# A weight scan's loads: issued by GpSimd into shared tiles, or by ScalarE into four tiles of its own

## The chip, the cores and the metric

The kernel runs on one core of one Trainium2 chip. The metric is the device time of one execution in microseconds (us). A core has five engines that run side by side, each in its own order: TensorE (PE in the profile; its weight loads are PEld), VectorE (DVE), ScalarE (ACT), GpSimd (POOL) and SyncE (SP). They meet at semaphores. Transfers between HBM and the on-chip memory are issued by SP, POOL or ACT, go into the issuing engine's own queue, and are then moved by the core's 16 DMA engines, which all queues share. An engine that has to wait before it issues a transfer holds up everything behind it in its own order.

## What is computed

Two layers of a diffusion backbone, on 1024 latent tokens and 256 context tokens of width 1024. Each layer is a mixer followed by a feed-forward part with gate, up and down weights (hidden width 2816 = 22 blocks of 128). Cut to what matters:

```python
def ada_mod(cond, w, b):
    m = (jax.nn.silu(cond) @ w + b)[..., None, :]
    return jnp.split(m, 6, axis=-1)

def swiglu(u, w_gate, w_up, w_down):
    return (jax.nn.silu(u @ w_gate) * (u @ w_up)) @ w_down
...
for i in range(DEPTH):
    sh1, sc1, g1, sh2, sc2, g2 = ada_mod(c, ada_w[i], ada_b[i])
    ...
    h_lat = h_lat + g2 * swiglu(modulate(rms_norm(h_lat, norm2_g[i]), sh2, sc2),
                                ffn_w_gate[i], ffn_w_up[i], ffn_w_down[i])
return rms_norm(h_lat, final_g)
```

## The kernel before

The program is one straight list of instructions for each engine. The code below is run once, tile by tile; a scheduler then sets each engine's order, hands out the slots of the tile pools and puts in the semaphore waits. `self.follow(ins)` ties what is issued inside it behind `ins` on the same engine.

**The stage.** The change acts in the feed-forward part of the first layer, method `ffn(0, ...)`. Its gate and up products of the latent tokens are done in Strassen-Winograd form: a loop over 11 units `i`, each with two blocks of 128 hidden features. A unit has 7 products for gate and 7 for up (`wino_steps`), each product 12 matmuls of 128x512 in f16 (line 1983), so 168 matmuls. VectorE and ScalarE make the weight operands of a unit: ScalarE the scaled high part (line 1842), VectorE the remainder (line 1843), VectorE the sums of weight blocks (lines 1961 to 1969). ScalarE copies partial results out of PSUM (line 1988) and applies Silu (lines 2127, 2129). VectorE adds partial results (lines 1997, 2007, 2012), multiplies gate by up and forms the sums for the next matrix product (lines 2084 to 2090, method `finish`). For the down weights of a unit, VectorE makes four sums (lines 2044 to 2047, method `sums`).

**Three side jobs** are woven into the units, so as to use engines that have room:

- `scan`: the second layer's gate and up weights (44 blocks of 128x1024) are read once, to get a sum of absolute values for each, from which their f16 scale follows later. Each block is loaded into a tile and ScalarE takes Abs with an accumulated sum (line 1813). It keeps four blocks ahead, and `ffn` advances it four times in a unit.
- `ada_group`, called `todo` in `ffn`: the modulation vectors `silu(c) @ ada_w`. A block of 128x1024 of `ada_w` is loaded by GpSimd, and VectorE takes four dot products with it (line 565, two for `c_ctx` and two for `c`), here called a **dot group**. Units 0 to 7 do three such blocks, the later ones two.
- `finish` and `sums` write their results to DRAM (`d<-g`, `d<-tk`, `d<-s`) by GpSimd, through `ldr`, line 338.

**The shared tiles.** Scan blocks and `ada_w` blocks both live in the pool `p4` (`S4()`, tag `s4`, shown as `s` in the profile), which has 21 tiles of 128x1024 f32. In this stage 14 of them hold the layer's input operands (28 pairs of 128x512 in f16, two pairs a tile), 2 hold the conditioning vectors, and 5 are left. The scheduler gives a tile that comes free to whichever request stands next, and the request waits for the tile's last reader.

**The order on GpSimd.** All loads of the two jobs and all the writes stand in one row on GpSimd, and each waits there for its own tile or its own data.

```python
self.p4 = ent(tc.tile_pool(name="p4", bufs=21))
def lda(self, out, in_):
    self.nc.scalar.dma_start(out, in_)
def ldr(self, out, in_):
    self.last_ldr = self.nc.gpsimd.dma_start(out, in_).ins
```

Below, line 347 is the plain matmul of `mm`, lines 351 and 353 are `split`, 332, 335 and 338 are the issues of `ld` (SP), `lda` (ACT) and `ldr` (POOL).

Of the kernel before, what the change touches and what calls it, by code (L numbers as in the profile page):

```python
# [13 lines left out]
AF = mybir.ActivationFunctionType  # L14
# [244 lines left out]
class Builder:  # L259
# [1536 lines left out]
        nc.vector.tensor_scalar(ad[:, m * 8:m * 8 + 16], ad[:, m * 8:m * 8 + 16], t[:, 1:2], None, op0=MUL)  # L1796
        self.xinv = t[:, 0:1]

    def scan(self, key, tiles, ahead=4):

        nc = self.nc
        n = len(tiles)
        sums = self.C(2 * n)
        st = []
        for k in range(n + ahead):
            if k < n:
                t = self.S4()
                self.ldr(t, tiles[k])
                st.append(t)
            if k >= ahead:  # L1810
                t, i = st.pop(0), k - ahead
                with self.follow(self.last_hi):
                    nc.scalar.activation(t, t, AF.Abs, accum_out=sums[:, i:i + 1])
            yield
        self.wsc[key] = sums

# [1159 lines left out]
```

## Time and profile before

| what | value |
|---|---|
| time, median of 3 | 2927.53 us (2925.7 and 2940.76 the others) |
| the profiled execution's own time | 2929.4 us |
| its span in the profile | 2927.6 us |
| PE busy | 2759.0 us, 94% |
| VectorE busy | 2100.2 us, 72% |
| ScalarE busy | 1428.6 us, 49% |
| GpSimd busy | 565.0 us, 19% |
| mean granted clock of TensorE | 0.979 |

A row of the timeline is: start in us, length in us, engine, line, operation, out<-in, shape, count, and in brackets how long the engine had been idle and what ended that. A row of waits is: who waited, for whom, us in total, times, longest. A row of windows is: the stretch, its length, then busy time and instruction count of PE, PEld, DVE, ACT and POOL, the granted clock, the DMA engines' share and GB/s. By windows, the stretch before this stage (0 to 890 us) has 817.77 us of PE, the stretch of the down product behind it (1395 to 1610 us) 212.61 us in 215, and the second feed-forward part (2340 to 2927 us) 573.22 us in 587.

### The profile page before, as it was taken

To read this page: it belongs to the slowest core of one execution; us is meant where nothing else is said; L and a number is where in the kernel's file an instruction comes from. 1 tells how busy PE (TensorE), PEld (TensorE's weight loads), DVE (VectorE), ACT (ScalarE), POOL (GpSimd) and SP (SyncE) were. 2 spreads that over 40 slices of the span, in tenths; PEclk is the share of its full clock that TensorE was granted. 3 is DMA by queue.
4 is the path that set the end of the run, shared out by engine and by line. 5 is a ranking of instruction groups with operands and counts; after the bars stand their busy time and mean duration, and the time that the engine had idled before them with its cause. 6 is when DMAs were issued, how large, how long until landed. Compare 5 with 4: busy or idle time off the path is not lost. (4 is left out here: it accounts for less than half of the span.)

```text
span 2927.6 us, 43743 instructions
## 1 busy us (share of the span) xinstructions
PE 2759.0 (94%) x15570; PEld 1999.4 (68%) x15570; DVE 2100.2 (72%) x3683; ACT 1428.6 (49%) x2445; POOL 565.0 (19%) x921
## 2 busy tenths in 40 slices
PE   7999888999999988889999999999999999999998
PEld 3877677788896433334787988898987444444887
DVE  5678788768777776777778635787877876775546
ACT  3434235442685433345346434777865553443434
POOL 1210234341001212123111001333322012222000
PEclk9999999999999999999999999999999999999999
DMA  7355546755655655568997534878875335665664
GB/s 257 108 159 178 164 134 197 242 185 195 239 169 198 227 200 198 201 234 302 336 311 251 159 130 119 194 189 195 202 236 196 115 126 191 223 207 202 229 194 137
DMA packets 304936, 580.42 MB, mean 198 GB/s; under 512 B 82760, under 2 KB 129546, under 8 KB 304718
## 3 DMA queue, kind: packets, MB, share of 16 engines
q1 hardware_dynamic: 234894, 367.34, 40.1%
q0 software_dynamic: 66976, 205.57, 20.6%
q10 hardware_dynamic: 2848, 4.72, 0.4%
q8 instruction: 123, 2.02, 0.3%
q14 instruction: 95, 0.78, 0.1%
HBM read 430.17 MB, written 119.80 MB: 188 GB/s over the span
## 5 line engine op out<-in xcount | busy, mean ns | idle before, releaser
L1983 PE MATMUL ps<-s,s 128*128 128x512 f16 x2280 | 528.9, 387 | 60.9 <-ACT tk L1988 29.4
L1983 PEld LDWEIGHTS <-s 128*128 128x128 f16 x2640 | 260.5, 99 | 392.8 <-issue 73.3
L347 PE MATMUL ps<-s,wh 128*128 128x256 f32 (+1 forms) x1784 | 414.1, 334 | 8.2 <-ACT wh L351 5.3
L347 PEld LDWEIGHTS ps<-s,wh 128*128 128x128 f32 x1784 | 300.5, 191 | 43.3 <-ACT wh L351 6.8
L347 PE MATMUL ps<-s,wl 128*128 128x256 f32 (+1 forms) x892 | 273.0, 332 | 5.8 <-DVE wl L353 5.8
L351 ACT CAST s<-s 128x1024 fp32r<-128x1024 f32 (+2 forms) x192 | 172.7, 927 | 201.3 <-DMA s<-d 183.7
L2177 PE MATMUL ps<-s,s 128*128 128x512 f32 (+1 forms) x1000 | 258.2, 384 | 3.6 <-DVE s L353 3.3
L347 PE MATMUL pq<-s,wh 128*128 128x512 f32 (+1 forms) x840 | 255.2, 384 | 0.3 <-ACT wh L351 0.3
L347 PE MATMUL ps<-s,s 128*128 128x65 f16 (+4 forms) x2748 | 228.1, 234 | 14.9 <-DMA s<-tk 4.8
L353 DVE TENSOR_TENSOR s<-s,s 128x1024 fp32r<-128x1024 f32 (+2 forms) x170 | 190.7, 1154 | 70.3 <-ACT s L351 70.0
L1983 PE MATMUL ps<-s,hl 128*128 128x512 f16 x924 | 216.6, 385 | 1.2 <-ACT hl L1842 1.2
L2177 PEld LDWEIGHTS ps<-s,s 128*128 128x128 f32 x1000 | 184.3, 188 | 42.8 <-DVE s L353 6.4
L353 DVE TENSOR_TENSOR wl<-ws,wh 128x1024 fp32r<-128x1024 f32 (+1 forms) x102 | 121.4, 1192 | 120.7 <-ACT wh L351 116.2
L338 POOL DMA_DIRECT2D d<-s x245 | 133.3, 545 | 380.4 <-DVE s L1699 87.5
L1983 PEld LDWEIGHTS <-hl 128*128 128x128 f16 x1056 | 104.5, 99 | 129.6 <-issue 7.6
L351 ACT CAST wh<-ws 128x1024 fp32r<-128x1024 f32 (+1 forms) x102 | 103.5, 1016 | 168.0 <-PE ps L347 89.1
L347 PEld LDWEIGHTS ps<-s,wl 128*128 128x128 f32 x892 | 168.1, 192 | 24.4 <-DVE wl L353 7.6
L347 PEld LDWEIGHTS pq<-s,wh 128*128 128x128 f32 x840 | 149.3, 189 | 22.3 <-ACT wh L351 1.1
L347 PE MATMUL pq<-s,wl 128*128 128x512 f32 (+1 forms) x420 | 158.8, 378 | 0.0
L1842 ACT ACTIVATE s<-t,c 128x512 f16<-128x512 f32 x176 | 117.6, 713 | 71.8 <-DVE t L1962 54.9
L2177 PE MATMUL ps<-s 128*128 128x512 f32 (+1 forms) x500 | 149.5, 386 | 0.6 <-ACT s L351 0.6
L347 PEld LDWEIGHTS ps<-s,s 128*128 128x128 f32 (+1 forms) x828 | 129.3, 192 | 26.8 <-ACT t L2513 3.2
(523 smaller groups left out, 5385.0 us busy)
## 6 DMA issues: line engine op xcount, KB each, us to landing
s<-d SPq DMA_DIRECT2D x283, 256.0 KB, 4.1
d<-s POOLq DMA_DIRECT2D x229, 256.0 KB, 3.9
s<-in_down SPq DMA_DIRECT2D x150, 256.0 KB, 6.2
s<-in_ada_w POOLq DMA_DIRECT2D x64, 512.0 KB, 6.1
ws<-in_up SPq DMA_DIRECT2D x44, 512.0 KB, 4.3
ws<-in_gate SPq DMA_DIRECT2D x42, 512.0 KB, 3.7
d<-s SPq DMA_DIRECT2D x60, 256.0 KB, 2.3
d<-g POOLq DMA_DIRECT2D x56, 256.0 KB, 3.4
```

Of the source, the lines that this page charges most:

```text
L338: self.last_ldr = self.nc.gpsimd.dma_start(out, in_).ins
L347: self.last_mm = self.nc.tensor.matmul(o, l, r, start=st, stop=sp).ins
L351: self.last_hi = nc.scalar.copy(hi, src).ins
L353: self.last_lo = eng.tensor_tensor(lo, src, hi.bitcast(F32), SUB).ins
L1842: self.last_hi = self.nc.scalar.activation(hi, src, AF.Copy, scale=s).ins
L1983: nc.tensor.matmul(ps, x[:, sl], y, start=first and j == 0 and x is wh and y is xh, stop=j == 3 and x is wl, skip_group_check=True)
L2177: m = nc.tensor.matmul(acc[j][:, c0:c1], x[:, sl], y[:, xs], start=first and k == 0, stop=last and k == 2, skip_group_check=True)
```

## The change

`scan` takes four tiles of the pool once, at its start, and goes round them. A block's load is issued by ScalarE (`lda`, line 335), behind the Abs that read the tile's previous block, and inside the same `follow` as the Abs. The parameter `ahead` goes; four blocks ahead stay four. Nothing else is edited; the method is two lines shorter, so that lines behind it count two less (line 1843 becomes 1841, 565 stays).

```diff
-    def scan(self, key, tiles, ahead=4):
+    def scan(self, key, tiles):
...
-        st = []
-        for k in range(n + ahead):
-            if k < n:
-                t = self.S4()
-                self.ldr(t, tiles[k])
-                st.append(t)
-            if k >= ahead:
-                t, i = st.pop(0), k - ahead
-                with self.follow(self.last_hi):
-                    nc.scalar.activation(t, t, AF.Abs, accum_out=sums[:, i:i + 1])
+        st = [self.S4() for _ in range(4)]
+        for k in range(n + 4):
+            t = st[k % 4]
+            with self.follow(self.last_hi):
+                if k > 3:
+                    nc.scalar.activation(t, t, AF.Abs, accum_out=sums[:, k - 4:k - 3])
+                if k < n:
+                    self.lda(t, tiles[k])
             yield
```

The instructions of the engines move with it. GpSimd's row in the middle of the stage, before (`in_gate` is a scan load, `in_ada_w` a load for a dot group, `d` a write to DRAM):

```order
L338 DMA s_2637_10629<-in_gate 128x1024
L338 DMA s_2639_10662<-in_gate 128x1024
L338 DMA d_7414<-s_2582_10374 128x512
L338 DMA s_2644_10721<-in_gate 128x1024
L338 DMA d_7416<-s_2557_10153 128x512
L338 DMA s_2649_10740<-in_ada_w 128x1024
L338 DMA d_7418<-tk_10388 128x512
L338 DMA s_2654_10750<-in_ada_w 128x1024
```

The same place on GpSimd after the change:

```order
L338 DMA d_7412<-g_10258 128x512
L338 DMA s_2638_10734<-in_ada_w 128x1024
L338 DMA d_7415<-tk_10288 128x512
L338 DMA d_7414<-s_2571_10363 128x512
L338 DMA d_7416<-s_2549_10145 128x512
L338 DMA d_7418<-tk_10377 128x512
L338 DMA s_2643_10744<-in_ada_w 128x1024
```

The scan loads are gone from the row, and the `in_ada_w` loads stand between writes alone. The load for the unit's first dot group, `s_2633`, stands four rows ahead of `s_2638` and waits for the last dot group of the unit before.

VectorE after the change, at the same unit, from the end of the first dot group (on `s_2633`) to the start of the second (on `s_2638`):

```order
L565 ISA s_2633_10724,c_99<-s_2633_10724,s_2360_9153,ah_10731 128x512
L565 ISA c_99 128x1
L1841 SCALAR_TENSOR_TENSOR hl_10843<-ws_10839,c_9148,hl_10843 128x1024
L2085 TENSOR_TENSOR tk_10288<-s_2549_10145,g_10258 128x512
L1995 TENSOR_TENSOR tk_10614<-ps_10650,tk_10614 128x512
L2086 TENSOR_TENSOR s_2571_10363<-g_10320,tk_10288 128x512
L2088 TENSOR_TENSOR s_2549_10145<-g_10320,s_2549_10145 128x512
L2082 TENSOR_TENSOR s_2605_10471<-tk_10614,s_2605_10471 128x512
L2087 TENSOR_TENSOR tk_10377<-s_2565_10272,s_2571_10363 128x512
L565 ISA t_10737,ah_10736<-s_2638_10734,s_2361_9156,c_101 128x512
```

Before, the first dot group stood behind these seven operations; now it stands ahead of them, and they lie between the first group and the second. Between the second and the third there are three sums of `down` weights (lines 2042 to 2044), where before there were one to three operations.

ScalarE after the change, at the same unit:

```order
L1809 ACTIVATE s_2393_9238,c_9234<-s_2393_9238 128x1024
L335 DMA s_2390_9235<-in_gate 128x1024
L1840 ACTIVATE hl_10843<-ws_10839,c_9148 128x1024
L1986 COPY g_10584<-ps_10458 128x512
L335 DMA s_2391_9236<-in_gate 128x1024
L335 DMA s_2392_9237<-in_gate 128x1024
L335 DMA s_2393_9238<-in_gate 128x1024
L1986 COPY tk_10614<-ps_10601 128x512
L1986 COPY s_2621_10598<-ps_10458 128x512
```

Before, the same copies and the scaled high part `hl` followed the four Abs directly. Now four issues stand among them.

## The prediction, on record before the run

> **What bounds the kernel now.** I read the chain of waits first. Its steps start at 2027 us, so it says nothing of this change's stage, and its shares add to only about a third of the span:
>
> ```profile
> PE 25%; DVE 3%; DMA 1%; issue 1%; ACT 1%; SPq 0%; POOL 0%; DVEq 0%; ACTq 0%; POOLq 0%
> ```
>
> So I cut the stage out with the timeline, by the first sum of `down` weights (line 2044), which VectorE makes once a unit, and then asked for the windows between such marks.
>
> ```profile
> 939.89 0.69 DVE L2044 TENSOR_TENSOR s<-s,s 128x512 f32<-128x512 f32 x1
> 1021.53 0.69 DVE L2044 TENSOR_TENSOR s<-s,s 128x512 f32<-128x512 f32 x1
> 1311.72 0.69 DVE L2044 TENSOR_TENSOR s<-s,s 128x512 f32<-128x512 f32 x1
> ```
>
> ```profile
> 939.89:1021.53 81.64, 76.72 (x347) 34.13 (x346) 63.16 (x115) 35.72 (x59) 18.32 (x34) 0.98 0.65 226
> 1021.53:1311.72 290.19, 238.43 (x1009) 102.27 (x1007) 208.06 (x386) 113.11 (x188) 59.76 (x111) 0.92 0.61 205
> 1311.72:1395.00 83.28, 83.28 (x386) 39.94 (x385) 62.87 (x108) 42.97 (x70) 29.91 (x56) 1.00 0.87 308
> ```
>
> Between the first two marks lie two units, between the second and the third six. Behind the third PE is never idle: 386 matmuls in 83.28 us, 0.2157 us each, so a unit of 168 matmuls needs 36.2 us of PE. The six in the middle take 290.19 / 6 = **48.4 us** each, at a granted clock of 0.92. This is the one stretch here that PE does not bound. Who is late there is in the waits of VectorE and PE in that window:
>
> ```profile
> DVE t L565 <- DMA s<-in_ada_w: 71.1, 17, 10.7
> DVE tk L2007 <- ACT tk L1988: 3.8, 3, 1.3
> DVE hl L1843 <- ACT hl L1842: 3.0, 5, 0.8
> DVE s L565 <- DMA s<-in_ada_w: 2.3, 2, 1.7
> ```
>
> ```profile
> PE ps L1983 <- ACT tk L1988: 27.6, 6, 5.7
> PE ps L1983 <- DVE s L2007: 13.5, 5, 5.4
> PE ps L1983 <- ACT s L1842: 10.5, 6, 3.0
> ```
>
> VectorE stands 73.4 us before dot groups, until their `in_ada_w` tile has landed. PE waits 51.6 us for results that VectorE or ScalarE has late behind that. VectorE's busy 208.06 / 6 = 34.7, its dot-group waits 73.4 / 6 = 12.2 and its other waits (3.8 + 3.0, and 0.5 in rows of 0.3 and less) 1.2 add up to 48.1: **a unit is as long as VectorE's row**, 35.9 us and what it waits for `in_ada_w`.
>
> **Why those tiles are late.** One unit, GpSimd first, then VectorE:
>
> ```profile
> 1085.41 0.54 POOL L338 DMA_DIRECT2D s<-in_gate  x1
> 1098.84 0.54 POOL L338 DMA_DIRECT2D s<-in_gate  x1 [4.18 <-ACT s L1813]
> 1102.25 0.53 POOL L338 DMA_DIRECT2D s<-in_ada_w  x1
> 1118.36 0.53 POOL L338 DMA_DIRECT2D s<-in_ada_w  x1 [15.04 <-DVE c L565]
> 1125.95 0.54 POOL L338 DMA_DIRECT2D s<-in_ada_w  x1 [4.20 <-DVE c L565]
> ```
>
> ```profile
> 1084.89 0.08 DVE L565 DVE_READ_ACCUMULATOR2_ANT c<- 128x1 f32 x1
> 1114.57 0.75 DVE L565 CUSTOM_DVE_ANT_0 t<-s,s,c 128x512 f32<-128x512 f32 x1 [10.54 <-DMA s<-in_ada_w]
> 1122.63 0.75 DVE L565 CUSTOM_DVE_ANT_0 t<-s,s,c 128x512 f32<-128x512 f32 x1 [1.79 <-DMA s<-in_ada_w]
> 1125.57 0.08 DVE L565 DVE_READ_ACCUMULATOR2_ANT c<- 128x1 f32 x1
> 1130.64 0.75 DVE L565 CUSTOM_DVE_ANT_0 t<-s,s,c 128x512 f32<-128x512 f32 x1 [4.38 <-DMA s<-in_ada_w]
> ```
>
> The dot group that ends at 1084.9 frees its tile, and half a microsecond later a *scan* load takes it. The next `in_ada_w` load gets the tile of the last scanned block, and so is issued only at 1102.25, behind three scan loads that waited for the Abs. It lands in the burst of that moment, 12.3 us later. The other two go one at a time through that one tile: issued 0.3 us behind a dot group, landed in 4.3 and 4.7 us.
>
> **The change, part by part.**
>
> *First dot group.* Four tiles of the five belong to the scan, one to the dot groups. So the load for a unit's first group is issued when the last group of the unit before ends, and on GpSimd only writes stand ahead of it. By the order, 17 operations of VectorE lie between: eleven sums and copies of 128x512, at the 0.60 us a start of the rows below, five products of line 1843 of that size, at the 0.66 of the row of three below (1.99 us), and one of 128x1024, 1.20: 11.1 us. The load leaves 0.3 us behind the group and ahead of the burst, as today's second and third, which land in 4.3 and 4.7 us: I take a wait of **0**. It can't be less; at the 12.3 us of the slowest load it is 12.3 + 0.3 - 11.1 = 1.5.
>
> *Second dot group.* Between it and the first stand one 128x1024 operation and six of 128x512:
>
> ```profile
> 1094.93 1.28 DVE L1843 SCALAR_TENSOR_TENSOR hl<-ws,c,hl 128x1024 f16<-128x1024 f32 x1
> 1096.13 2.07 DVE L1843 SCALAR_TENSOR_TENSOR s<-t,c,s 128x512 f16<-128x512 f32 x3
> ```
>
> ```profile
> 1098.12 0.69 DVE L2088 TENSOR_TENSOR s<-g,tk 128x512 f32<-128x512 f32 x1
> 1098.72 0.69 DVE L2090 TENSOR_TENSOR s<-g,s 128x512 f32<-128x512 f32 x1
> ```
>
> From start to start 1.20 and 0.60, so 1.20 + 6 x 0.60 = 4.8 us. The load leaves 0.3 us behind the first group and needs 4.3 to 12.3 us: a wait of 0 to 7.8. Which, is set by the burst, for at this place the four scan loads now go out on ScalarE's queue. In the burst around 1102 the loads took:
>
> ```profile
> s<-in_gate POOLq DMA_DIRECT2D x3, 512.0 KB, 8.1
> s<-in_down SPq DMA_DIRECT2D x4, 256.0 KB, 14.3
> ws<-in_up SPq DMA_DIRECT2D x1, 512.0 KB, 8.6
> s<-in_ada_w POOLq DMA_DIRECT2D x1, 512.0 KB, 12.3
> ```
>
> A load of 512 KB that was first in its own queue took 8.6 us and the scan loads ahead of `in_ada_w` 8.1; the 12.3 is the one that stood behind them in the same queue. That queue now holds no scan load, so I take 8 us: a wait of 8.0 + 0.3 - 4.8 = **3.5**.
>
> Here the Trainium skill speaks against the change. Its page "DMA: Bandwidth & Descriptors", section "Issuing engines are not separate DMA queues", says that transfers of all engines run on the same 16 DMA engines and interleave, so that another issuing engine saves only issue time. By that rule the second load stays at the burst's end, the first rival below. The trace bears out that they share (the two SP rows are as slow as the POOL ones); it does not show a third queue in such a burst.
>
> *Third dot group.* Three sums lie between, 0.72 us from start to start:
>
> ```profile
> 1118.70 0.69 DVE L2045 TENSOR_TENSOR s<-s,s 128x512 f32<-128x512 f32 x1
> 1119.43 0.69 DVE L2046 TENSOR_TENSOR s<-s,s 128x512 f32<-128x512 f32 x1
> ```
>
> So 2.2 us. With 4.3 to 4.7 us of landing the wait is 2.4 to 2.8; behind a still running burst up to 10.4. The load stands where today's third stands, so I take **2.5**.
>
> *Together* a unit waits 6.0 in place of 12.2 (bounds 2.4, and 1.5 + 7.8 + 2.5 = 11.8), and is 35.9 + 6.0 = **41.9 us** long (38.3 to 47.7). The six units gain 6 x (48.4 - 41.9) = **39 us** (4 to 61). PE's own 36.2 us stay below that, so VectorE remains the bound. The two units ahead, 40.8 us each with 4.9 us of PE idle in both, give 0 to 5; I take 2.
>
> *GpSimd* loses 44 issues and *ScalarE* gets them, at the prices of these rows:
>
> ```profile
> L338 POOL DMA_DIRECT2D s<-in_gate x22: 527/538/542, 893.9 to 1149.7; - x22
> L335 ACTq DMA_DIRECT2D d<-s x16: 326/326/961, 1450.4 to 1608.7; - x16
> ```
>
> GpSimd's 44 x 0.538 = 23.7 us count as nothing: it is busy 59.76 of 290.19 us. ScalarE's 44 x 0.326 = 14.3 us are 1.3 us a unit; it is busy 113.11 of 290.19 us, and that idle time hides them. Behind the issues stand the split `hl` and the copies that PE waits for; if the cover were gone and each issue took the longest row's 0.96, it would be 3.8 us a unit, the second rival. What an issue waits for (its tile's Abs, just ahead) is over by then.
>
> *The end of the stage.* The last four blocks are now loaded only when four Abs have freed the tiles, and the last four Abs then wait for a landing, with casts for the next stage and a copy of PSUM behind them on ScalarE. Before, they ran on without a wait:
>
> ```profile
> 1363.27 1.06 ACT L1813 ACTIVATE s<-s 128x1024 f32<-128x1024 f32 x1
> 1364.32 0.57 ACT L1988 COPY g<-ps 128x512 f32<-128x512 f32 x1
> ```
>
> The copy comes 4 to 8 us later by the landings above. By the order, 26 matmuls (5.6 us) lie on PE between what the copy reads and what waits for it. I take 2 us of loss (0 to 8), once.
>
> *Sum*: 39 + 2 - 2 = 39 us off 2929.4 of the profiled execution gives 2890; that execution was 1.9 us above the median of the runs shown, so **2888 us**. The forecast's own range, from 4 slower (a gain of 4 and a tail of 8) to 66 faster (61 and 5), is 2862 to 2932.
>
> **The rivals.** A measurement of this kernel can tell about 0.5% (14.6 us) from no change.
>
> *The burst decides, not the queue* (0.12): the second load lands as late as the first does today, 12.3 us behind its issue, and the third in the burst's tail; the waits add up to 10.3 (with 2.5) to 12.2 again. For it: the DMA share is 0.61 over the window though units are long, and the same bytes must go in a shorter unit. Against it: two of today's three loads, in the same unit, land in 4.3 to 4.7 us. It gives 0 to 13 off, some **2922**. That the change then does nothing of weight is this case too.
>
> *ScalarE becomes late* (0.10, the slower side): its row is in order, and PE already waits 27.6 us for its copies. If each issue costs 0.96 us on the path of `hl` and the copies, 11 units lose 42 us, and if the dot groups wait as today this is up to 2970, some **2950** at half of it. It decides from 6.2 us a unit, what the waits give back: 1.6 us an issue if they do give it. Against it: its 39% busy and the 0.326 median.
>
> *PE becomes the bound* (0.08): the second wait is gone, the third is hidden in PE's lead, units take 36.2 us: 6 x 12.2 + 5 = 78 off, **2850**.
>
> **How the numbers follow.** My forecast has 0.70; about 0.05 of it, the long waits, falls within 0.5%. Faster 0.65 + 0.08 = 0.73, same 0.05 + 0.12 = 0.17, slower 0.10. The likeliest case gives 2888. The range takes in its bounds, most of the first rival and a little of the third, 2858 to 2932; about 0.17 is left out, the slower case and most of PE's.
>
> **What would show it.** The marks of line 2044 should stand some 42 us apart. The first dot group of a unit should find its tile landed, the second wait 0 to 8 us and the third 2 to 3; VectorE's wait for `in_ada_w` over the six units should fall from 73 to near 36 us, PE's 51.6 us of waits to less than half, and the granted clock there rise from 0.92. A second dot group that still waits 7 us or more speaks for the first rival; waits of PE for ScalarE's `hl` and copies that grow, with VectorE on time, for the second. I am wrong in the mechanism if units stay at 48 us with the dot groups on time, and wrong in the place if the stage shrinks and the time behind it grows.

## The result, and the profile after

| | before | after |
|---|---|---|
| time, median (4 runs each) | 2927.59 us | 2896.75 us |
| ratio | | 0.9891, 95% interval 0.9851 to 0.9932 |
| the profiled execution's own time | 2929.4 us | 2895.0 us |

The change makes the kernel 1.1% faster, 31 us; 39 were forecast. Two more measurements of the same pair, below, gave ratios of 0.9887 (0.9869 to 0.9905) and 0.9882 (0.9864 to 0.9900).

The marks of the `down` sums, now line 2042, in the timeline of the changed kernel (start, length, engine, line):

```profile
937.22 0.69 DVE L2042 TENSOR_TENSOR s<-s,s 128x512 f32<-128x512 f32 x1
1019.11 0.68 DVE L2042 TENSOR_TENSOR s<-s,s 128x512 f32<-128x512 f32 x1
1266.52 0.69 DVE L2042 TENSOR_TENSOR s<-s,s 128x512 f32<-128x512 f32 x1
```

The windows between them, and from the last mark to the first product into `pq` and from there to the end (length, then busy time of PE, PEld, DVE, ACT and POOL, granted clock, DMA share, GB/s):

```profile
937.22:1019.11 81.89, 76.95 (x343) 34.02 (x341) 66.55 (x127) 36.36 (x60) 15.19 (x28) 0.96 0.69 238
1019.11:1266.52 247.41, 229.21 (x1026) 101.70 (x1025) 205.93 (x387) 111.93 (x184) 47.69 (x88) 0.97 0.70 245
...
1266.52:1378.70 112.18, 108.67 (x495) 60.62 (x493) 74.60 (x122) 50.54 (x78) 31.26 (x58) 1.00 0.85 298
1378.70:2892.80 1514.10, 1474.06 (x8977) 1099.39 (x8975) 1049.00 (x1761) 784.22 (x1378) 243.87 (x429) 0.99 0.63 193
```

The same two last stretches of before:

```profile
1311.72:1422.70 110.98, 110.32 (x502) 61.36 (x501) 80.32 (x135) 50.89 (x77) 36.52 (x68) 1.00 0.90 325
1422.70:2927.60 1504.90, 1467.31 (x8977) 1094.64 (x8975) 1048.29 (x1760) 782.11 (x1378) 242.87 (x429) 1.00 0.63 193
```

Stretch by stretch: up to the first mark 2.7 us gained, the two units behind it 0.3 lost, the **six units 42.8 gained** (41.2 us each in place of 48.4), the rest of the stage 1.2 lost, and everything behind it **9.2 lost**. The last is the surprise, since nothing was edited there; the same 8977 matmuls had 6.8 us more of PE busy time.

The marks are set by VectorE's written order, which the change moved: 1009 matmuls lie between the last two marks before, 1026 after. Over the same 1008 matmuls the six units took 290.5 us before and 243.9 after (48.4 and 40.7 each), 46.6 gained; the two ahead of them then lost 1.2, and the rest of the stage 3.0.

Who waits in the six units (who, for whom, us in total, times, longest):

```profile
DVE t L565 <- DMA s<-in_ada_w: 39.5, 11, 5.0
PE ps L1981 <- ACT tk L1986: 14.2, 6, 2.9
PE ps L1981 <- DVE s L2005: 4.0, 5, 1.4
```

VectorE's wait for `in_ada_w` fell from 73.4 to 39.5 us, PE's waits from 51.6 to 18.2. One unit shows how, first GpSimd's loads, then VectorE's dot groups:

```profile
1059.07 0.54 POOL L338 DMA_DIRECT2D s<-in_ada_w  x1 [7.59 <-DVE c L565]
1068.17 0.54 POOL L338 DMA_DIRECT2D s<-in_ada_w  x1 [2.67 <-DVE c L565]
1086.66 0.54 POOL L338 DMA_DIRECT2D s<-in_ada_w  x1
```

```profile
1063.29 0.75 DVE L565 CUSTOM_DVE_ANT_0 t<-s,s,c 128x512 f32<-128x512 f32 x1 [2.46 <-DMA s<-in_ada_w]
1078.91 0.75 DVE L565 CUSTOM_DVE_ANT_0 t<-s,s,c 128x512 f32<-128x512 f32 x1
1095.99 0.75 DVE L565 CUSTOM_DVE_ANT_0 t<-s,s,c 128x512 f32<-128x512 f32 x1 [4.99 <-DMA s<-in_ada_w]
```

These are a third, a first and a second group in the order of the prediction: 2.46, 0 and 4.99 us of waiting. The load for the second group leaves at 1086.66, 2.5 us behind the last of the scan's four issues (1084.16, below), and lands 9.3 us later.

ScalarE at the same place. A row of ACTq is an issue, a row of ACT an operation; a bracket would show idle time ahead of it:

```profile
1081.81 1.04 ACT L1809 ACTIVATE s<-s 128x1024 f32<-128x1024 f32 x1
1082.76 0.19 ACT L1809 ACTIVATION_READ_ACCUMULATOR s<-s 128x1 f32 x1
1082.85 1.04 ACT L1809 ACTIVATE s<-s 128x1024 f32<-128x1024 f32 x1
1083.25 0.82 ACTq L335 DMA_DIRECT2D s<-in_gate  x2
1083.80 0.19 ACT L1809 ACTIVATION_READ_ACCUMULATOR s<-s 128x1 f32 x1
1083.89 1.14 ACT L1840 ACTIVATE hl<-ws,c 128x1024 f16<-128x1024 f32 x1
1084.16 0.39 ACTq L335 DMA_DIRECT2D s<-in_gate  x1
1084.93 0.56 ACT L1986 COPY g<-ps 128x512 f32<-128x512 f32 x1
```

No operation stands idle ahead of its start: the issues pass beside the operations that are running.

### The profile page after: what moved, and what is told of

Same layout as the page of the kernel before. It is cut to its first block, busy times and chain, and to the rows that moved or that the text cites. A ratio compares the mean times of both kernels' runs of the same rounds, so it can differ in the third digit from the quotient of the medians.

```text
span 2892.9 us, 43698 instructions
## 1 busy us (share of the span) xinstructions
PE 2752.6 (95%) x15570; PEld 1999.5 (69%) x15570; DVE 2095.6 (72%) x3683; ACT 1430.1 (49%) x2445; POOL 543.3 (19%) x877
## 3 DMA queue, kind: packets, MB, share of 16 engines
q1 hardware_dynamic: 234894, 367.34, 40.7%
## 5 line engine op out<-in xcount | busy, mean ns | idle before, releaser
L1981 PE MATMUL ps<-s,s 128*128 128x512 f16 x2280 | 520.8, 384 | 29.1 <-ACT tk L1986 18.2
```

Of the source, the lines that this page charges most:

```text
L1981: nc.tensor.matmul(ps, x[:, sl], y, start=first and j == 0 and x is wh and y is xh, stop=j == 3 and x is wl, skip_group_check=True)
```

## The experiments

All are edits of the changed kernel unless said otherwise. The first four ran on one chip, the other eight on a second one, in two sessions of four; each ratio is to runs of the kernel before in the same session. The last column times the same 1008 matmuls of the stage in every trace, beginning with the one that starts at 1021.6 us in the first profile of before; between the marks lie 985 to 1057 matmuls, as VectorE's written order has it.

| run | what | median us | ratio to before, 95% interval | six units by the marks, us each | the same 1008 matmuls, us a unit |
|---|---|---|---|---|---|
| after_again | changed kernel | 2897.56 | 0.9887 (0.9869 to 0.9905) | 41.7 | 41.3 |
| tiles_only | own tiles, GpSimd's queue | 2889.35 | 0.9854 (0.9833 to 0.9875) | 41.3 | 40.4 |
| queue_only | shared tiles, ScalarE's queue | 2913.15 | 0.9951 (0.9932 to 0.9970) | 46.4 | 45.8 |
| two_for_dots | one tile more in the pool | 2901.43 | 0.9904 (0.9889 to 0.9920) | 38.1 | 39.2 |
| before_again | kernel before | 2934.75 | 1.0025 (1.0007 to 1.0043) | 47.6 | 47.3 |
| half_act | fourth scan tile of two halves | 2880.97 | 0.9842 (0.9817 to 0.9868) | 37.8 | 38.8 |
| half_pool | the same, GpSimd's queue | 2885.87 | 0.9851 (0.9829 to 0.9874) | 38.3 | 39.3 |
| no_scan | no scan loads, no Abs | 2863.42 | 0.9771 (0.9757 to 0.9785) | 35.4 | 36.3 |
| after_third | changed kernel | 2898.32 | 0.9882 (0.9864 to 0.9900) | 41.8 | 41.0 |
| tiles_again | as tiles_only | 2884.75 | 0.9842 (0.9822 to 0.9862) | 41.1 | 40.3 |
| half_act_again | as half_act | 2881.63 | 0.9824 (0.9801 to 0.9847) | 37.9 | 38.8 |
| abs_only | all Abs, 4 of 44 loads | 2877.07 | 0.9821 (0.9790 to 0.9852) | 40.0 | 38.2 |

before_again sets the kernel before against itself: 1.0025, with an interval that leaves out 1. A difference of that size, 7 us, between two runs is therefore not taken as shown.

### Is the loss behind the stage the change's?

The changed kernel and the kernel before, unedited.

> The changed kernel once more, for a closer time and a second profile. Up to the end of the stage the profile of the changed kernel stands 44 us ahead of the one of before (1422.7 against 1378.7 us at the first product of line 2177, now 2175, into pq); at the end it is 34.5 us ahead. Theory A (the loss of 9 us behind the stage comes from stretches at half clock that fall now here, now there): the six middle units take 40.5 to 42 us each again, the halved stretches at 1600, 1904, 2245 and 2320 us are not all at the same places, and the time is anywhere from 2885 to 2900. Theory B (the change itself brings on what is lost behind the stage): the same lead of 44 at the end of the stage, again 34 to 36 at the end, with the same places of half clock, time 2893 to 2899.

> The kernel before once more, for a second profile. In the first one, 1504.9 us lie from the first product into pq of line 2177 to the end, and one stretch of 3.4 us at half clock in them (2264 us); in the changed kernel 1514.2 and 1513.9 us, with five and three such stretches. Theory A (accident of one profile): this time 1509 to 1516 us from that product to the end, with three or more halved stretches, and the units at 48 us as before. Theory B (the change lengthens what comes behind its stage): 1503 to 1507 us again, one or two halved stretches.

The places of half clock in these two texts are counted from the zero of the trace's clock record, which is 10.4 to 10.6 us ahead of the zero of the profile's rows. Windows of the second profile of before, the six units and what lies behind the first product into `pq`:

```profile
1018.90:1304.30 285.40, 239.17 (x1017) 102.85 (x1015) 207.63 (x386) 115.28 (x191) 59.77 (x111) 0.92 0.61 208
...
1414.00:2928.00 1514.00, 1475.24 (x8978) 1100.33 (x8976) 1048.09 (x1760) 782.70 (x1377) 243.03 (x429) 0.99 0.63 192
```

Now the kernel *before* needs 1514.0 us behind the stage, with as much PE busy time as the changed kernel (1475.24 and 1474.06), and its six units are 4.8 us shorter. So the loss of 9.2 us was an accident of the first profile, and theory A holds of the two kernels together. In after_again the loss behind came again (1513.9 us), with three stretches of half clock in place of five, two of them at the same places of the program as two of the five; before_again had five there, three of them at the program places of the changed kernel's. They are not peculiar to the change. Two runs of one unchanged kernel scatter as much: half_act and half_act_again, the same program, needed 1519.3 and 1507.9 us behind that product. The two profiles of before have nearly the same span, 2927.6 and 2928.0 us, made of different parts.

Over all profiles, two of before and three of the changed kernel (2892.9, 2897.1 and 2897.2 us), the means differ by 32.1 us: six units 38.4 gained, two units ahead of them 0.8, up to the first mark 0.5 lost, rest of the stage 2.2 lost, behind it 4.5 lost, of which before's first profile alone makes 4.4. Over the same matmuls the six units gained 41.3, the two ahead 0.3, and the rest of the stage lost 3.2.

### The tiles or the queue?

Each half of the change alone. tiles_only and tiles_again:

```diff
-                    self.lda(t, tiles[k])
+                    self.ldr(t, tiles[k])
```

queue_only, against the kernel before:

```diff
                 t = self.S4()
-                self.ldr(t, tiles[k])
+                self.lda(t, tiles[k])
```

> The scan's four own tiles, but its loads on GpSimd's queue as before. Theory T (the shared tiles were the cause, the queue is nothing): the first dot group waits 0, the second some 5 and the third 2.5 us as in the changed kernel; six middle units of 41 to 42 us, time 2890 to 2900. Theory Q (the queue matters too): the load of the second dot group stands behind four scan loads in GpSimd's queue, which themselves wait for their Abs; it lands 12.3 us or more behind its place and the group waits 8 us or more; units of 44 to 47 us, time 2905 to 2922.

> The scan's loads on ScalarE's queue, but tiles taken in turn from the shared pool as before. Theory T: the first dot group's load still takes the tile of the last scanned block and comes as late as before, waits of 9 us or more a unit remain; and a scan load that waits for a tile which a dot group holds now stands in ScalarE's row ahead of the split products that PE waits for, so that PE's waits for ScalarE grow: units of 47 us or more, time 2920 to 2960. Theory Q: the burst no longer stands ahead of the dot groups' loads in their queue, and most of the gain is there, units of 42 to 44, time 2893 to 2910.

Waits in the six units of queue_only:

```profile
DVE t L565 <- DMA s<-in_ada_w: 55.2, 17, 7.6
...
DVE s L565 <- DMA s<-in_ada_w: 4.6, 2, 2.7
...
PE ps L1983 <- ACT s L1842: 22.4, 6, 6.8
PE ps L1983 <- ACT tk L1988: 12.9, 6, 5.8
```

With shared tiles the dot groups still wait 59.8 us, and PE's wait for ScalarE's split products (line 1842) grew from 10.5 to 22.4 us. The load for a unit's first group still takes the tile of the last scanned block and waits for its Abs:

```profile
1101.39 0.55 POOL L338 DMA_DIRECT2D s<-in_ada_w  x1 [0.58 <-ACT s L1813]
```

It leaves 16.9 us behind the end of the dot group ahead of it (17.3 in the unit of before shown in the prediction), so both waits that theory T named were there. But these loads landed in 8.7 to 10.1 us in the six units, against 9.7 to 13.1 before, and the dot groups' waits fell by 13.6 us in all, more than PE's wait for the split products grew. The median, 17 us below before, lies between the two forecasts, 7 us under T's range and 3 above Q's; so do the units. By the medians the queue alone gave about half of the change's gain. Own tiles alone gave all of it and more. **The tiles are the cause; with them the queue is not needed.** (Own tiles move VectorE's written order too, as shown ahead of the prediction; no run has the one without the other.) What theory Q said of tiles_only falls by GpSimd's rows in tiles_again, and the dot group that they feed:

```profile
1075.15 0.54 POOL L338 DMA_DIRECT2D s<-in_gate  x1 [3.04 <-ACT s L1809]
1076.19 0.55 POOL L338 DMA_DIRECT2D s<-in_gate  x1 [0.50 <-ACT s L1809]
1077.23 0.53 POOL L338 DMA_DIRECT2D s<-in_gate  x1 [0.49 <-ACT s L1809]
1078.27 0.53 POOL L338 DMA_DIRECT2D s<-in_gate  x1 [0.51 <-ACT s L1809]
1079.89 0.55 POOL L338 DMA_DIRECT2D d<-g  x1 [1.09 <-DVE g L2082]
1080.83 0.53 POOL L338 DMA_DIRECT2D s<-in_ada_w  x1 [0.39 <-issue]
```

```profile
1085.12 0.69 DVE L2005 TENSOR_TENSOR s<-ps,s 128x512 f32<-128x512 f32 x1
1090.35 0.75 DVE L565 CUSTOM_DVE_ANT_0 t<-s,s,c 128x512 f32<-128x512 f32 x1 [4.54 <-DMA s<-in_ada_w]
```

Behind four scan loads in the same queue the load lands 9.5 us after its issue (1080.83 to 1090.35); with the scan's loads in ScalarE's queue it was 9.3. Over the six units such loads took 8.9 to 11.4 us, mean 9.8, in the two profiles of own tiles on GpSimd, and 7.3 to 9.9, mean 9.0, in the three of the changed kernel. That is the rule of the Trainium skill weighed in the prediction (page "DMA: Bandwidth & Descriptors", section "Issuing engines are not separate DMA queues"): transfers of all issuers interleave on the same DMA engines. Here the traces agree with it in the main: with a second queue the landing was 0.8 us shorter with own tiles, and some 2 us shorter with shared ones (means of 9.2 in queue_only and 11.3 before).

### Does ScalarE's queue even cost something?

tiles_only was 8 us faster than after_again. Both once more, side by side:

> The changed kernel beside its twin with GpSimd's loads on one chip. Theory E (ScalarE's issues are not free: the first two units took 81.9 and 83.0 us with them, 78.0 with GpSimd's): this is 5 to 10 us slower than the twin, as on the first chip (2897.6 against 2889.4), two first units of 81 to 84 us. Theory F (accident): the two lie within 4 us of each other, 2889 to 2898 both.

> The twin: four own tiles, loads on GpSimd's queue. Theory E: 2886 to 2892, two first units of 77 to 79.5 us. Theory F: 2889 to 2898, two first units of 78 to 83 us as they fall.

2898.32 against 2884.75 us: theory E's difference is there, 13.6 us where it said 5 to 10. From the first mark to the first product into `pq` the twin is 7.9 us faster in both pairs of profiles. But the issuing itself shows no cost: those rows pass beside ScalarE's operations, as shown above. VectorE's waits from the first mark to the last, after_third and then tiles_again:

```profile
DVE t L565 <- DMA s<-in_ada_w: 56.5, 15, 5.4
```

```profile
DVE t L565 <- DMA s<-in_ada_w: 48.5, 15, 5.5
```

The 8 us are in the dot groups' waits (in the first pair 58.6 and 49.6). The written order of VectorE's row differs between the two kernels: in the twin, eight operations lie between a first and a second group, the sum of line 2005 that PE waits for among them (1085.12 above, ahead of the wait), and four or five between a second and a third; in the changed kernel, in its six units, six or seven, with that sum behind the wait, and mostly three, in one unit none. Fewer operations cover less of a landing. That this order, and not something else in ScalarE's issuing, makes the 8 us is read from the rows; no run moved the order alone.

### What is left of the waits

One tile for three loads a unit is still few. two_for_dots gives the dot groups a second one by pool sizes:

```diff
-        self.p4 = ent(tc.tile_pool(name="p4", bufs=21))
-        self.p2 = ent(tc.tile_pool(name="p2", bufs=35))
+        self.p4 = ent(tc.tile_pool(name="p4", bufs=22))
+        self.p2 = ent(tc.tile_pool(name="p2", bufs=33))
```

> As the changed kernel, but with one tile more in the pool of 128x1024 tiles (22, the pool of 128x512 tiles 33 in place of 35 to make room), so that the dot groups have two. Theory T: each load is issued one dot group earlier, all three waits fall to 0 to 1 us, VectorE's row needs 35 us and PE 36.2: six middle units of 36.5 to 38 us, 20 to 28 us less than the changed kernel, time 2866 to 2880, if two 128x512 tiles less cost nothing. Rival (the burst decides, whatever the tiles): the second load still lands late, units of 40 us or more, time above 2888. Rival 2: the smaller pool makes loads of down weights late and gives a part back, which would show as new waits of VectorE for in_down.

```profile
DVE hl L1841 <- ACT hl L1840: 19.2, 5, 4.5
DVE t L565 <- DMA s<-in_ada_w: 6.3, 5, 1.8
```

In the stage theory T was nearly right: 6.3 us of waiting, and units of 38.1 us by the marks, 39.2 over the same matmuls, where it said 36.5 to 38. The total was not: 2901 us where it said 2866 to 2880. The first mark stood at 947.5 us, 10 later than in the changed kernel; but it stood at 948.7 and 945.1 in half_act and abs_only too, which keep the pools, and at 940.6 in the second run of half_act, so this is scatter. Behind the stage it took 1530.1 us, where the other profiles have 1505 to 1521. By the medians it is 20 us slower than half_act. That the smaller pool costs this is likely but not shown; the waits of VectorE for `in_down` that rival 2 named do not occur. half_act keeps the pools and takes the scan's fourth tile as two halves instead:

```diff
-        sums = self.C(2 * n)
-        st = [self.S4() for _ in range(4)]
+        sums = self.C(2 * n)
+        rest = sums[:, n:n + n // 4]
+        st = [(self.S4(),) for _ in range(3)] + [(self.S2(), self.S2())]
...
+        nc.vector.tensor_tensor(sums[:, 3:n:4], sums[:, 3:n:4], rest, ADD)
```

> As the changed kernel (loads on ScalarE), but the scan's fourth tile is two tiles of 128x512 from their own pool, so that the dot groups have two tiles of 128x1024 and no pool changes size; one load of the four becomes two of half the size, and one Abs two. Theory T: units of 37.5 to 39 us as in the run with 22 tiles, whose 10 us lost ahead of the stage are not lost here; first product into pq at 1360 to 1366 us, time 2875 to 2886. Rival (the pool of 128x512 tiles is short in this stage too): loads of down weights come late, units of 40 us or more, time 2890 or more.

> The same with the loads on GpSimd's queue. If the issuing queue is nothing for the burst, as own tiles with GpSimd's loads showed (units of 41.28 against 41.24 and 41.69), this has the same units as its twin on ScalarE, 37.5 to 39 us, and a time within 0.4% of it, likelier below, since the two first units were 4 us shorter with GpSimd's loads; 2868 to 2886. If GpSimd's row is what the dot groups' loads then wait in, units of 40 us or more.

> The variant with two tiles for the dot groups once more, on this chip. It was 2881.0 where the changed kernel was 2896.8 and 2897.6. Theory T: again 12 to 20 us below the changed kernel, units of 37.5 to 38.5 us. If what it gained hung on the chip or the profile, within 6 us of it.

Windows and waits of half_act_again in its six units:

```profile
1019.50:1247.00 227.50, 219.48 (x1000) 98.25 (x999) 198.48 (x375) 110.00 (x193) 45.95 (x85) 0.99 0.75 259
```

```profile
DVE hl L1845 <- ACT hl L1844: 18.8, 6, 4.6
DVE t L565 <- DMA s<-in_ada_w: 6.1, 5, 1.7
```

Both times, on the same chip, the median fell where T had it, in the last session 16.7 us below the changed kernel, though the first product into `pq` came at 1370.7 us in the first profile, behind T's 1360 to 1366 (1362.6 in the second). At 2881 us it beats both kernels and has the lowest median of the versions that compute everything; but it is not told apart from its twin on GpSimd's queue, half_pool (0.9851 and 0.9842, overlapping intervals), nor from tiles_again, the twin with one tile for the dot groups (2884.75 in the same session, 3 us). By the marks its six units are 19 us shorter than those of tiles_again, over the same matmuls 9.5, and at the first product into `pq` it is 9 us ahead. That profile is of one of its two fastest executions (2872.24 us), so the medians keep less. VectorE's next wait has come forward too, for `hl` from ScalarE.

Is the second wait the burst, or ScalarE's work? no_scan leaves out the scan, its loads and its Abs, and sets the row sums of the second layer's weights to 1; abs_only keeps the 44 Abs and leaves out 40 of the loads:

```diff
-                if k < n:
+                if k < 4:
                     self.lda(t, tiles[k])
```

> The changed kernel without the scan's loads and without its Abs: the row sums of the second layer's gate and up weights are left out and set to 1. The dot groups then have all five tiles. Theory C (what is left of the second wait, 4.0 to 5.6 us a unit, is the burst that the scan's loads make): every load lands in 4 to 6 us and no dot group waits over 1 us; PE's own 36.2 us bound the units, 36.2 to 37.5 us. Theory D (the loads of down and gate weights on SP's queue make the burst by themselves): dot-group loads still take 7 us and more. Time 2862 to 2880 by C.

> The changed kernel with all 44 Abs but with only the first four of the scan's 44 loads: the row sums are of the first four blocks over and over. Without loads and Abs the kernel took 2863 us. Theory C (the loads' burst is what is left of the second wait): the dot groups' loads take 4 to 6 us, the second wait falls from 4.0 to 5.6 us to under 1.5, units of 37 to 39 us (the third wait of 2 us remains, for here the dot groups have one tile), time 2870 to 2885. Theory G (ScalarE's four Abs a unit, 4.4 us, are what holds PE): units of 40 us or more and PE's waits for ScalarE's copies as in the changed kernel, 14 us over six units, time above 2888.

The same 1008 matmuls in no_scan and in abs_only (a window also counts those cut by its ends), then waits between the marks of abs_only:

```profile
1011.90:1229.40 217.50, 217.50 (x1009) 98.59 (x1008) 203.08 (x384) 87.08 (x134) 45.42 (x84) 1.00 0.62 209
```

```profile
1026.10:1255.20 229.10, 220.50 (x1010) 98.68 (x1009) 200.66 (x381) 109.63 (x180) 45.88 (x85) 0.99 0.60 200
```

```profile
PE ps L1981 <- ACT tk L1986: 6.2, 3, 2.8
...
DVE t L565 <- DMA s<-in_ada_w: 31.6, 11, 4.1
```

Without the scan PE is never idle in these units, at a granted clock of 1.00, and the dot groups wait for no load (each lands in 3.7 to 5.0 us): this is the stage's floor, 36.3 us a unit, and the time is 33 us below the changed kernel. (By the marks a unit comes out at 35.4 us, less than PE needs, because only 985 matmuls lie between them.) With the Abs alone the second wait is 1.3 to 2.5 us in place of 4.0 to 5.0 and its load lands in 4.6 to 6.0 us, so **the burst of the scan's loads is most of the second wait**. The median, 2877.07, lies in theory C's range, and so do the units, 38.2 us; the 40.0 by the marks has 1057 matmuls in it. C had the second wait under 1.5 us and the third at 2; the third is 3.3 to 4.1, because in this written order one operation (once two) lies between the second and the third group. Theory G falls: with all Abs in place PE waits 6.2 us for the copies, not 14.

## Why the prediction was right, and what it missed

- *The bound*: a unit as long as VectorE's row. Right: 34.3 us busy (205.93 / 6), 6.6 of waits for `in_ada_w` and 0.3 other make 41.2. Busy time and all waits add up to the stretch for any engine; that VectorE is the bound lies in its waits, nearly all for loads that its own dot groups release and none for PE. The 41.9 of the forecast came close by two small misses that cancel: the waits are 0.6 us longer than its 6.0, and VectorE's other waits, kept at 1.2, fell to 0.3.
- *First group, 0*: 0.0 in every unit.
- *Second group, 3.5 (0 to 7.8)*: 4.0 to 5.0. The landing was taken as 8 us; it measured 7.3 to 9.3 in the first profile after.
- *Third group, 2.5*: 1.4 to 4.2, mean 2.7.
- *Six units, 39 off*: 42.8 between the two first profiles, 38.4 over all of them; over the same matmuls 46.6 and 41.3.
- *Two units ahead, 2 off*: 0.3 lost, 0.8 gained over all profiles: close to nothing, the lower end of its 0 to 5.
- *ScalarE's and GpSimd's issues, nothing*: right for the issues themselves, and the second rival did not occur: PE's wait for the copies fell from 27.6 to 14.2 us, and in the unit shown no operation of ScalarE waits behind an issue. What the placement does cost, 8 to 14 us against the twin, is not in these terms.
- *End of the stage, 2 lost*: 1.2, and 2.2 over all profiles (3.0 and 3.2 over the same matmuls). Two of the last four Abs waited, 1.8 us together.
- *The burst rival*: half true. The burst decides how late the second load lands, with little difference by the queue that issues it (means of 9.0 and 9.8 us), as the rule behind that rival says; but the rival's waits of 10.3 to 12.2 a unit did not follow, because the tile, which is what the change frees, sets *when* the first and third loads leave. The prediction credited the queue with a landing of 8 in place of 12.3. Own tiles without the queue come to 9.8, and the time is no worse.
- *PE as the bound*: not reached by the change; no_scan shows it as the floor.

Between the first two profiles the terms of the stage add up to 41 us off (42.8 - 0.3 - 1.2), over all profiles to 37, where 39 were forecast; the time moved by 31. What was missed is the step that took the sum off the profiled execution of before (2929.4) as if that were typical, because its total stood 1.9 us from the median. Its parts were not: the first product into `pq` came 8.5 us later than in the second profile, and what lies behind took 9 us less. In the other four of the five profiles of the two kernels this rest took 1514 us; with those 9 us the 2888 become 2897, and 2896.75 was measured. That this comes out so exactly is luck: it is worked out afterwards, from two profiles of before, and the profiles of the other runs scatter by more than 10 us there.

The clock belongs to this. In the six units it rose from 0.92 to 0.97: the clock record has ten stretches at half rate there before and four after. All of its stretches in this stage are 3.4 or 6.8 us long in the profiles of the two kernels. The Trainium skill (page "TensorE: Matmul & The Clock Gate", section "Part 1: The HAM clock gate") says that the array falls to half rate after an idle window of about 3.4 us; lengths of one and two such windows agree with it. The waits of PE at which the four of the changed kernel begin do not: they are 2.0 to 2.9 us long, shorter than such a window. That waits bring the stretches on is read from this: each of the fourteen begins inside a wait of PE or within 1 us of its end, fewer and shorter waits went with fewer stretches, and no_scan, with no waits, has none in these units.

## What to carry to other kernels

Where two streams of loads take tiles in turn from one pool, each waits for the other's last reader: look at whose release lets the late load leave, and give the stream that holds up the bounding engine its own tiles. Another issuing engine is no sure gain on top: here it gave 17 us with shared tiles and cost 8 to 14 with own ones. Once the tiles are apart, count how many operations lie between a load's release and its use, since a second tile buys a whole group of them. And take two profiles before pricing a gain from parts of one: totals within 0.5 us hid stretches that differed by 9.

## What the runs showed of the hardware that was not expected

- A 512 KB load that landed alone in 3.7 to 5 us took 7.3 to 11.4 behind a burst of four others and the weight loads: a mean of 9.8 in the burst's own queue (tiles_only, tiles_again) and of 9.0 in another one (the changed kernel, three profiles).
- ScalarE's issues of scan loads (0.33 to 0.54 us in the changed kernel) run while its operations go on; four of them per unit left no gap in its row.
- The same 8977 matmuls behind the stage had PE busy times between 1467 and 1480 us in different executions (two_for_dots had the most; the two runs of half_act, one program, 1475 and 1468), with one to seven stretches of 3.4 or 6.8 us at half clock, at places of the program that recurred only in part.
- In the changed kernel, waits of PE of 2.0 to 2.9 us were enough for a stretch of 3.4 us at half clock.
